# The two products of a chunked recurrence: odd chunks written to the other half of the partitions

## The chip, the cores and the metric

The kernel runs on one core of one Trainium2 chip. The metric is the device time of one execution in microseconds (us), the median of the runs shown. A profile is one further execution with the hardware profiler on; its own time is given beside it. PE is the matrix engine (TensorE), PEld its loading of weights, DVE the vector engine, ACT the scalar engine, POOL the GpSimd engine, SP the engine that issues most of the transfers.

## The reference, cut to what matters

One transformer block over 1024 positions and a width of 1024, in float32: a token mixer with two branches, softmax attention with forget gates (8 heads of 64) and an RWKV-7 recurrence (8 heads of 64), merged by gates, and then a convolutional feed-forward layer of width 2816. The change lies in the recurrence:

```python
def step(state, inp):
    r_t, w_t, k_t, v_t, a_t, b_t = inp
    sa = jnp.einsum('bhvk,bhk->bhv', state, a_t)
    state = state * w_t[:, :, None, :] + sa[..., None] * b_t[:, :, None, :] + v_t[..., None] * k_t[:, :, None, :]
    y_t = jnp.einsum('bhvk,bhk->bhv', state, r_t)
    return state, y_t

_, y = lax.scan(step, state0, (tm(r_h), tm(w_h), tm(k_h), tm(v_h), tm(a_vec), tm(b_vec)))
```

## The kernel before, in words

The recurrence is not run step by step. The sequence is cut into chunks of 64 positions (CH). A unit of work is one pair of heads `p` and one half `hf` of the sequence: 8 chunks (NCU) and two heads `h`, of which one stands on partitions 0 to 63 and the other on 64 to 127 (`HS[0]` and `HS[1]`). There are 4 pairs and 2 halves, so 8 units.

For each unit `pre` (from line 698) makes what belongs to the chunks alone: the masked products of keys, `E` (line 764); the inverse of a triangular matrix for each chunk, by substitution in blocks of 32 rows, 31 steps of two DVE instructions each (`t` and `E`, lines 784 and 786) between transfers through DRAM (`sm` to `M32` before them, `se` to `TT` behind them); transposes of values and queries into `UV` and `QA`; and `q` (line 822), whose matmuls read one half of the partitions and write the other.

`main` (from line 830) then finishes the unit:
- `xi` and `zi` (lines 850 and 857) complete the inverse; ACT copies the result into `TT` (line 859).
- The product with the inverse, `uw` (line 868): for each chunk and head a matmul of 64 rows, 64 output rows and 128 columns, `TT` by `QA`. Four chunks fill one PSUM bank of 512 columns, so two banks hold the unit. DVE copies the second half of each chunk's columns into `Wt` (line 870), ACT the first half into `UV` (line 872).
- The product of the step matrices, `mz` (line 880), of the same shapes: `Wt` by `E`. DVE adds to make `Zt` (line 882) and the step matrices `Mt` (line 884).
- `sp` and `yp` (lines 893 and 895) start the sums of states and outputs; they read `UV` and `E`.
- The walk over the chunks (lines 899 to 905): `sp` by `Mt` and the state before, and ACT makes the next state `S` (line 903).
- `yp` by `Zt` (line 910), and the group norm of the outputs (`mu`, `va` and what follows).

The banks of `uw`, `mz`, `xi`, `zi` and other short products come from one pool of four, `gen`. Every f32 matmul appears in the profile as two records.

Around this, PE's order is written out beforehand: `Weave` (line 49) counts a time for PE from a cost for each matmul (`mm_cost`, line 68), which goes by the shapes and types of the operands alone. `main` and `pre` are generators; a `yield` of a number asks that so many nanoseconds of other PE work be put in before the chain goes on, and that work is the projections (`ps_rkv`, `qk`, `v`, `gt`), which have banks of their own. Only PE's order is fixed by hand in this stage. The orders of DVE, ACT, POOL and SP are made by the scheduler of the language, from its own model of times. Behind the recurrence come the attention and the feed-forward layer.

Of the kernel before, what the change touches and what calls it, by code (L numbers as in the profile page):

```python
# [12 lines left out]
ALU = mybir.AluOpType  # L13
# [9 lines left out]
CH = 64  # L23
NCU = NH // CH
# [108 lines left out]
def hybrid_block(ctx: ExitStack, tc: tile.TileContext, a, out):  # L133
    nc = tc.nc
# [3 lines left out]
    def mm(o, lhsT, rhs, start, stop, more=False):  # L138

        weave.mm_cost(o, lhsT, rhs)  # L140
        nc.tensor.matmul(o, lhsT, rhs, start=start, stop=stop, skip_group_check=more)  # L141
# [8 lines left out]
    tt, stt, ts = nc.vector.tensor_tensor, nc.vector.scalar_tensor_tensor, nc.vector.tensor_scalar  # L150
# [195 lines left out]
    with ExitStack() as es:  # L346
# [7 lines left out]
        def gen(name):  # L354
            return pr.tile([128, NH], F32, tag="gen", name=name)
# [45 lines left out]
        HS = (slice(0, 64), slice(64, 128))  # L401
# [285 lines left out]
        Mt = rw.tile([128, NCU, 128], F32, name="Mt")  # L687
# [142 lines left out]
        def main(k, p, hf):  # L830
            o = units.pop((p, hf))
            n = f"{p}_{hf}"
            cs = slice(hf * NH, hf * NH + NH)
            pcd, ar, E, QA, TT, bon, UV = (o[k] for k in ("pcd", "ar", "E", "QA", "TT", "bon", "UV"))
# [25 lines left out]

            yield 2000
            Wt = rw.tile([128, NCU, CH], F32, tag="Wt", name=f"Wt{n}", bufs=1)
            for c0 in range(0, NCU, 4):
                ps = gen(f"uw{n}{c0}")
                for c in range(c0, c0 + 4):
                    for h in range(2):
                        x = (c - c0) * 128
                        mm(ps[HS[h], x : x + 128], TT[HS[h], c, :], QA[HS[h], c, :, :], start=True, stop=True)
                pv = ps.rearrange("p (c a s) -> p c a s", a=2, s=CH)
                nc.vector.tensor_copy(Wt[:, c0 : c0 + 4, :], pv[:, :, 1, :])  # L870
                for h in range(2):
                    nc.scalar.copy(UV[HS[h], c0 : c0 + 4, h, :], pv[HS[h], :, 0, :])
            yield 2970
            Zt = rw.tile([128, NCU, CH], F32, tag="Zt", name=f"Zt{n}", bufs=1)
            for c0 in range(0, NCU, 4):
                ps = gen(f"mz{n}{c0}")
                for c in range(c0, c0 + 4):
                    for h in range(2):
                        x = (c - c0) * 128
                        mm(ps[HS[h], x : x + 128], Wt[HS[h], c, :], E[HS[h], c, h, 1:3, :], start=True, stop=True)  # L880
                pv = ps.rearrange("p (c a s) -> p c a s", a=2, s=CH)
                tt(Zt[:, c0 : c0 + 4, :], pv[:, :, 0, :], ar[:, 1, c0 : c0 + 4, :], op=ALU.add)
                for h in range(2):
                    tt(Mt[HS[h], c0 : c0 + 4, HS[h]], pv[HS[h], :, 1, :],
                       ident[HS[h], HS[h]].unsqueeze(1).to_broadcast([64, 4, CH]), op=ALU.add)

            yp = py.tile([128, NCU, CH], F32, tag="yp", name=f"yp{n}")
# [87 lines left out]
        def main_chain():  # L975
            for k, (p, hf) in enumerate(order):
                while (p, hf) not in units:
                    yield 200
                yield from main(k, p, hf)
                yield 0  # L980
# [205 lines left out]
    def bank(k, name):  # L1186
        return pb.tile([128, NH], F32, tag="big", name=name) if k > 5 else pz.tile([128, NH], F32, tag=f"p{k}", name=name)
# [442 lines left out]
    ps = {t: [bank(k, f"wo{t}_{c}") for c, k in enumerate(ks)] for t, ks in enumerate(((0, 5), (6, 7), (1, 2)))}  # L1630
# [12 lines left out]
    def wo_do(t, k):  # L1643
        ps = [bank(k + c, f"wo{t}_{c}") for c in range(2)]
        for kt in range(KT):
            wo_mm(t, kt, ps)
        return ps

    ps = wo_do(3, 3)
# [7 lines left out]
    ps = wo_do(4, 0)  # L1657
# [15 lines left out]
    for t, k in ((5, 2), (6, 6), (7, 4)):  # L1673
        ps = wo_do(t, k)
# [229 lines left out]
    for s, k in enumerate(ORDER):  # L1904
        ps = banks[4:] if k in (7, 4, 2) else banks[0:4]
# [109 lines left out]
```

## Time and profile before

| what | value |
|---|---|
| median of 3 runs | 1662.81 us (1658.86 to 1663.45) |
| profiled execution, its own time | 1662.01 us |
| its span | 1660.2 us |
| mean granted clock | 0.989 |
| PE busy over the span | 1615.2 us (97%) |
| DVE busy over the span | 1223.2 us (74%) |
| ACT busy over the span | 822.3 us (50%) |

The profiled execution's own time is its span and 1.8 us around it. The first of the eight `uw` products begins at 235.4 us and the last at 576.6 us; the stretch from 230 to 606 us is the one to look at. A row of the order of time gives start, length, engine, line, operation, output and inputs, shapes and the number of records; a row of a tile gives the count and then shortest, median and longest duration in nanoseconds.

### The profile page before, as it was taken

The numbers are of one execution on the slowest core, as the hardware profiler recorded it, in microseconds if no ns is written. First come the engines' busy times: TensorE is split into PE (matmuls) and PEld (weight loads), VectorE is DVE, ScalarE is ACT, GpSimd is POOL, SyncE is SP. The second block draws the span as 40 slices with busy tenths as digits, with TensorE's granted clock in tenths as the row PEclk, the third lists the DMA queues.
The fourth block names the chain that finished last, engine by engine and source line by source line (L and its number), as shares of the span: only waits on it lengthen the run. The fifth ranks groups of instructions, "written<-read, shape, count | busy, mean of one in ns | idle before, by whom it ended". The sixth has DMA issues, their size and how long they took to land.

```text
span 1660.2 us, 25947 instructions
## 1 busy us (share of the span) xinstructions
PE 1615.2 (97%) x9694; PEld 1346.1 (81%) x9694; DVE 1223.2 (74%) x2371; ACT 822.3 (50%) x1540; POOL 130.3 (8%) x152
## 2 busy tenths in 40 slices
PE   7999999999999999999999999999999999999998
PEld 7777777898978788888778887888888888888886
DVE  5786787878876536888678347897777777786677
ACT  5563335444455656666623225654444444555455
POOL 0011001111111011221022000000000000000000
PEclk9999999999999999999999999999999999999999
DMA  8488645443343246433187411243223223574363
GB/s 336 139 322 238 177 116 140 131 121 97 100 115 97 96 129 153 124 114 110 64 323 265 166 70 58 66 138 108 96 95 120 97 96 108 208 266 156 125 209 108
DMA packets 121645, 240.59 MB, mean 145 GB/s; under 512 B 40048, under 2 KB 48880, under 8 KB 121520
## 3 DMA queue, kind: packets, MB, share of 16 engines
q1 hardware_dynamic: 113040, 220.58, 40.7%
q0 software_dynamic: 8480, 18.37, 4.2%
q8 instruction: 76, 1.25, 0.3%
q14 instruction: 49, 0.40, 0.1%
HBM read 173.35 MB, written 65.54 MB: 144 GB/s over the span
## 4 chain that ended last, share of the span: by engine, by line
PE 62%; DVE 3%; ACT 2%; DMA 1%; issue 1%; SPq 0%; ACTq 0%; DVEq 0%
PE X L141 14%; PE D L141 13%; PE Y L141 7%; PE wo L141 5%; PE br L141 5%; PE gt L141 4%; PE rk_ps L141 4%; PE W L141 3%; PE lg L141 2%; PE ov L141 2%; PE tp L145 2%; DVE nm L1049 1%; DVE P L1059 1%; DMA g<-d_gate 0%; DVE tl L1089 0%
## 5 line engine op out<-in xcount | busy, mean ns | idle before, releaser
L141 PE MATMUL D<-op,op 128*128 128x512 f32 x924 | 209.8, 389 | 0.0
L141 PEld LDWEIGHTS D<-op,op 128*128 128x128 f32 x924 | 173.3, 188 | 36.3 <-DVE op L1252 0.3
L141 PE MATMUL X<-T_m,S 128*128 128x512 f32 x440 | 106.9, 389 | 0.0
L141 PEld LDWEIGHTS X<-T_m,S 128*128 128x128 f32 x440 | 82.5, 188 | 17.5 <-ACT x L1542 0.4
L1251 ACT CAST op<-g 128x512 fp32r<-128x512 f32 x77 | 47.8, 621 | 72.1 <-PE D L141 47.8
L1252 DVE TENSOR_TENSOR op<-g,op 128x512 fp32r<-128x512 f32 x77 | 53.0, 688 | 41.1 <-ACT op L1251 41.1
L1502 DVE SCALAR_TENSOR_TENSOR c<-ab,vec,c 128x512 f32<-128x512 f32 x88 | 65.9, 749 | 18.4 <-ACT c L1505 16.8
L784 DVE TENSOR_TENSOR t<-E,M 128x60 f32<-128x60 f32 (+24 forms) x248 | 56.1, 226 | 26.6 <-DMA M<-sm 20.6
L274 DVE TENSOR_TENSOR lo_in<-raw_in,hi_in 128x512 fp32r<-128x512 f32 x84 | 57.7, 725 | 22.0 <-PE gt L141 7.2
L1466 DVE TENSOR_TENSOR A<-ur,A 128x512 fp32r<-128x512 f32 x64 | 43.9, 688 | 39.0 <-ACT A L1462 38.8
L1466 DVE TENSOR_TENSOR S<-ur,S 128x512 fp32r<-128x512 f32 x66 | 45.5, 691 | 35.2 <-ACT S L1462 35.1
L1462 ACT CAST S<-ur 128x512 fp32r<-128x512 f32 x66 | 41.0, 622 | 56.1 <-DVE ur L1455 30.9
L141 PE MATMUL Y<-T_h,S 128*128 128x512 f32 x264 | 65.6, 398 | 1.6 <-ACT T_h L1720 1.0
L141 PE MATMUL Y<-T_h,A 128*128 128x512 f32 x264 | 63.4, 389 | 0.0
L1053 ACT ACTIVATE P<-lg,nm 128x896 f32<-128x896 f32 (+3 forms) x64 | 47.4, 742 | 29.3 <-DVE nm L1049 19.6
L141 PEld LDWEIGHTS Y<-T_h,S 128*128 128x128 f32 x264 | 50.6, 192 | 13.4 <-ACT T_h L1720 1.8
L1462 ACT CAST A<-ur 128x512 fp32r<-128x512 f32 x64 | 39.6, 621 | 42.9 <-PE X L141 31.0
L141 PE MATMUL W<-B_f,A 128*128 128x512 f32 x252 | 60.6, 389 | 0.0
L786 DVE TENSOR_TENSOR E<-E,t 128x60 f32<-128x60 f32 (+24 forms) x248 | 55.8, 225 | 6.4
L141 PE MATMUL X<-B_b,A 128*128 128x512 f32 x252 | 60.5, 389 | 0.0
L141 PEld LDWEIGHTS Y<-T_h,A 128*128 128x128 f32 x264 | 49.5, 188 | 10.3
L272 ACT CAST hi_in<-raw_in 128x1024 fp32r<-128x1024 f32 x42 | 43.9, 1049 | 25.4 <-PE ps_rkv L141 11.3
(481 smaller groups left out, 4142.0 us busy)
## 6 DMA issues: line engine op xcount, KB each, us to landing
raw_in<-in_w_in SPq DMA_DIRECT2D x50, 512.0 KB, 3.9
wm<-in_w_mod SPq DMA_DIRECT2D x48, 512.0 KB, 6.7
ur<-in_w_up SPq DMA_DIRECT2D x44, 512.0 KB, 4.0
g<-d_g SPq DMA_DIRECT2D x35, 512.0 KB, 3.8
d_g<-gs SPq DMA_DIRECT2D x44, 256.0 KB, 2.0
d_g<-c SPq DMA_DIRECT2D x33, 256.0 KB, 4.3
d_st<-qh SPq DMA_DIRECT2D x64, 128.0 KB, 2.4
stA<-d_st POOLq DMA_DIRECT2D x8, 1024.0 KB, 6.2
```

The costliest lines, as they stand in the source:

```text
L141: nc.tensor.matmul(o, lhsT, rhs, start=start, stop=stop, skip_group_check=more)
L145: nc.tensor.transpose(o, i, eye)
L272: nc.scalar.copy(hi, raw)
L274: nc.vector.tensor_tensor(lo[:, c : c + NH], raw[:, c : c + NH], f32(hi[:, c : c + NH]), op=ALU.subtract)
L784: tt(tv, E32[:, 0:J, s : s + 1].to_broadcast([128, J, W]), M32[:, s : s + 1, s + 1 : 32].to_broadcast([128, J, W]), op=ALU.mult)
L786: tt(E32[:, 0:J, s + 1 : 32], E32[:, 0:J, s + 1 : 32], tv, op=ALU.add)
L1053: nc.scalar.activation(e[:, 0:n], lg[:, 0:n], AF.Exp, bias=nm[:, 0:1], accum_out=nm[:, 1:2])
L1251: nc.scalar.copy(hi, src)
L1252: tt(lo, src, f32(hi), op=ALU.subtract)
L1462: nc.scalar.copy(hi, src)
L1466: tt(lo, src, f32(hi), op=ALU.subtract)
L1502: stt(c, ab[:, x + hf * NH : x + hf * NH + NH], V("conv_w", 22 * x + i), c, op0=ALU.mult, op1=ALU.add)
```

## The change

In `uw` and in `mz` both banks are taken at the start, one for the even chunks and one for the odd ones, where before the first held chunks 0 to 3 and the second chunks 4 to 7. The matmuls of an even chunk write the half of the partitions that they read, as before; those of an odd chunk write the other half. The order of chunks and heads is the same, and so are the shapes. The evictions come after all 16 matmuls in the program. Those of an even chunk stay as they were but step over every second chunk; those of an odd chunk read one half of the partitions and write the other, and so `Wt` and `Zt` of the odd chunks take one instruction for each half: three instructions for a unit in place of two. `UV` and `Mt` already had one for each half; their number stays at four.

```diff
--- before.py
+++ after.py
@@ -860,28 +860,32 @@
 
             yield 2000
             Wt = rw.tile([128, NCU, CH], F32, tag="Wt", name=f"Wt{n}", bufs=1)
-            for c0 in range(0, NCU, 4):
-                ps = gen(f"uw{n}{c0}")
-                for c in range(c0, c0 + 4):
-                    for h in range(2):
-                        x = (c - c0) * 128
-                        mm(ps[HS[h], x : x + 128], TT[HS[h], c, :], QA[HS[h], c, :, :], start=True, stop=True)
-                pv = ps.rearrange("p (c a s) -> p c a s", a=2, s=CH)
-                nc.vector.tensor_copy(Wt[:, c0 : c0 + 4, :], pv[:, :, 1, :])
+            ps = [gen(f"uw{n}{e}") for e in range(2)]
+            for c in range(NCU):
                 for h in range(2):
-                    nc.scalar.copy(UV[HS[h], c0 : c0 + 4, h, :], pv[HS[h], :, 0, :])
+                    x = c // 2 * 128
+                    mm(ps[c % 2][HS[h ^ c % 2], x : x + 128], TT[HS[h], c, :], QA[HS[h], c, :, :], start=True, stop=True)
+            pv = [x.rearrange("p (c a s) -> p c a s", a=2, s=CH) for x in ps]
+            nc.vector.tensor_copy(Wt[:, 0::2, :], pv[0][:, :, 1, :])
+            for h in range(2):
+                nc.vector.tensor_copy(Wt[HS[h], 1::2, :], pv[1][HS[1 - h], :, 1, :])
+            for e in range(2):
+                for h in range(2):
+                    nc.scalar.copy(UV[HS[h], e::2, h, :], pv[e][HS[h ^ e], :, 0, :])
             yield 2970
             Zt = rw.tile([128, NCU, CH], F32, tag="Zt", name=f"Zt{n}", bufs=1)
-            for c0 in range(0, NCU, 4):
-                ps = gen(f"mz{n}{c0}")
-                for c in range(c0, c0 + 4):
-                    for h in range(2):
-                        x = (c - c0) * 128
-                        mm(ps[HS[h], x : x + 128], Wt[HS[h], c, :], E[HS[h], c, h, 1:3, :], start=True, stop=True)
-                pv = ps.rearrange("p (c a s) -> p c a s", a=2, s=CH)
-                tt(Zt[:, c0 : c0 + 4, :], pv[:, :, 0, :], ar[:, 1, c0 : c0 + 4, :], op=ALU.add)
+            ps = [gen(f"mz{n}{e}") for e in range(2)]
+            for c in range(NCU):
                 for h in range(2):
-                    tt(Mt[HS[h], c0 : c0 + 4, HS[h]], pv[HS[h], :, 1, :],
+                    x = c // 2 * 128
+                    mm(ps[c % 2][HS[h ^ c % 2], x : x + 128], Wt[HS[h], c, :], E[HS[h], c, h, 1:3, :], start=True, stop=True)
+            pv = [x.rearrange("p (c a s) -> p c a s", a=2, s=CH) for x in ps]
+            tt(Zt[:, 0::2, :], pv[0][:, :, 0, :], ar[:, 1, 0::2, :], op=ALU.add)
+            for h in range(2):
+                tt(Zt[HS[h], 1::2, :], pv[1][HS[1 - h], :, 0, :], ar[HS[h], 1, 1::2, :], op=ALU.add)
+            for e in range(2):
+                for h in range(2):
+                    tt(Mt[HS[h], e::2, HS[h]], pv[e][HS[h ^ e], :, 1, :],
                        ident[HS[h], HS[h]].unsqueeze(1).to_broadcast([64, 4, CH]), op=ALU.add)
 
             yp = py.tile([128, NCU, CH], F32, tag="yp", name=f"yp{n}")
```

## Prediction

> **What bounds the kernel now.** I read the page first, then the busy time of the stretch from 230 to 606 us, in which the recurrence runs, and after it the waits of that stretch.
>
> ```profile
> span 1660.2 us, 25947 instructions
> ...
> PE 1615.2 (97%) x9694; PEld 1346.1 (81%) x9694; DVE 1223.2 (74%) x2371; ACT 822.3 (50%) x1540; POOL 130.3 (8%) x152
> ```
>
> ```profile
> 230.00:606.00 376.00, 368.29 (x3651) 309.71 (x3650) 276.07 (x771) 188.88 (x368) 47.20 (x60) 1.00 0.39 110
> ```
>
> The numbers of the second row are length, then busy time of PE, PE's weight loads, DVE, ACT and POOL, and at the end the granted clock (1.00). PE stands still for 376.00 - 368.29 = 7.7 us of the stretch; whatever the recurrence leaves free, the woven-in projections fill. DVE has 100 us spare. So a microsecond taken from PE's own work is a microsecond of the whole, unless PE then meets a wait that does not move with it. The waits that it meets now are few:
>
> ```profile
> PE uw L141 <- ACT TT L859: 2.9, 2, 2.0
> PE v L141 <- DVE vs L955: 1.9, 3, 1.3
> PE sp L141 <- ACT S L903: 1.1, 1, 1.1
> ```
>
> (total, times, longest). None of them is for a PSUM bank of the two products, so taking both banks at the start of a product costs nothing that shows here.
>
> **The two products.** There are eight units (four head pairs, two halves), each with one uw and one mz product, 16 blocks in all:
>
> ```profile
> L141 PE MATMUL uw<-QA,TT x256: 269/269/418, 235.4 to 578.3; 64*64 64x128 f32 x128
> L872 ACT COPY UV<-uw x32: 344/367/369, 237.1 to 579.5; 64x256 f32<-64x256 f32 x32
> L870 DVE COPY Wt<-uw x16: 398/417/425, 236.7 to 578.6; 128x256 f32<-128x256 f32 x16
> ```
>
> ```profile
> L141 PE MATMUL mz<-E,Wt x256: 269/269/321, 240.7 to 583.6; 64*64 64x128 f32 x128
> L884 DVE TENSOR_TENSOR Mt<-mz,cst x32: 405/417/428, 242.2 to 585.7; 64x256 f32<-64x256 f32 x32
> L882 DVE TENSOR_TENSOR Zt<-mz,ar x16: 413/424/425, 241.9 to 584.9; 128x256 f32<-128x256 f32 x16
> ```
>
> 256 records in 8 units are 32 for 16 matmuls: an f32 matmul leaves two records, two passes. Here is one block in order of time (start, length):
>
> ```profile
> 235.41 1.96 PE L141 MATMUL uw<-QA,TT 64*64 64x128 f32 x32
> ...
> 236.69 0.42 DVE L870 COPY Wt<-uw 128x256 f32<-128x256 f32 x1
> ...
> 237.31 2.14 PE L141 MATMUL ps_rkv<-u_lo,hi_in 128*128 128x512 f32 x8
> ...
> 237.70 0.42 DVE L870 COPY Wt<-uw 128x256 f32<-128x256 f32 x1
> ```
>
> The last record starts 1.96 - 0.27 = 1.69 us after the first. Now the lucky place on which I rest most: in the seventh unit the product q, whose matmuls go from one half of the partitions to the other (the crossed pair of quarters), is directly followed by mz on the straight pair.
>
> ```profile
> 532.17 0.97 PE L141 MATMUL q<-UV,E 64*64 64x64 f32 x26
> ...
> 532.94 0.33 PE L141 MATMUL mz<-E,Wt 64*64 64x128 f32 x2
> 532.98 0.28 PE L141 MATMUL q<-UV,E 64*64 64x64 f32 x4
> ...
> 533.10 0.27 PE L141 MATMUL mz<-E,Wt 64*64 64x128 f32 x1
> ...
> 533.10 0.22 PE L141 MATMUL q<-UV,E 64*64 64x64 f32 x1
> 533.10 0.27 PE L141 MATMUL mz<-E,Wt 64*64 64x128 f32 x1
> ...
> 533.21 1.70 PE L141 MATMUL mz<-E,Wt 64*64 64x128 f32 x28
> ```
>
> Three things are in it. mz comes in pairs, the two quarters at once: two records at 532.94, two at 533.10, and then 28 records, 14 pairs, in steps of (1.70 - 0.27)/13 = 0.11. The first step is 0.16, since the first weight load lies open. And the last six records of q, on the crossed quarters, start at 532.98 to 533.11, after mz has begun: all four quarters run together, with q four records in 0.28 - 0.22 = 0.06 and mz's own steps no longer than elsewhere. The operands of q and mz share the rows of the array but not its columns. That such sharing costs nothing over many steps, and that two row halves can write two banks on the same partitions, these rows show:
>
> ```profile
> 242.81 0.29 PE L141 MATMUL yp<-E,UV 128*64 128x64 f32 x4
> 242.87 0.20 PEld L141 LDWEIGHTS sp<-UV,E 128*64 128x64 f32 x4
> 242.92 0.29 PE L141 MATMUL sp<-UV,E 128*64 128x64 f32 x4
> ...
> 256.58 1.16 PE L141 MATMUL p<-ar,bk 64*128 64x128 f32 x16
> ```
>
> sp and yp use two column halves over all rows and take 0.11 for four records of 64 columns; p uses two row halves over all columns, into two banks, and takes its 16 records of 128 columns in (1.16 - 0.27)/7 = 0.13 a pair with the open first load.
>
> **What the change saves on PE.** A block becomes eight rounds of four instead of 16 of two: the last round starts 0.16 + 6 x 0.11 = 0.82 after the first, and its second pair 0.01 later. Saved are 1.69 - 0.83 = 0.86 us a block, 16 x 0.86 = 13.8 us. The bounds are 0 (four quarters overlap only at such a seam) and 13.8 (the rounds cannot be shorter than one quarter's step); the seam shows the four together, so I take 13.8. The planner's cost of a matmul does not depend on the half it writes, so the order of PE's queue stays as it is.
>
> A rule of the Trainium skill speaks against this: its page TensorE: Matmul & The Clock Gate, in Part 3 (what overlaps and what doesn't), has matmuls start and end strictly in program order. By that rule the second pass of each matmul would hold back every later matmul, and the saving would be 0 in place of 13.8; the seam disagrees, since q's last six records start behind mz's first two.
>
> **What it adds.** One Wt copy and one Zt addition more in each unit, for the odd chunks have to change halves: 2 x 0.42 = 0.84 us of DVE, 6.7 in all, beside PE's work where there is room. ACT's four UV copies and DVE's four Mt additions stay in number and size. The even bank is full at 0.82 + 0.27 = 1.09 us into the block, exactly when the first bank (chunks 0 to 3) was before, so evictions begin as early; they end at most 0.42 later. But PE arrives at the next product 0.86 sooner. So each margin shrinks by 1.28 at the step from Wt to mz. The narrowest:
>
> ```profile
> 387.18 0.41 DVE L870 COPY Wt<-uw 128x256 f32<-128x256 f32 x1
> 434.83 0.42 DVE L870 COPY Wt<-uw 128x256 f32<-128x256 f32 x1
> 530.85 0.76 DVE L870 COPY Wt<-uw 128x256 f32<-128x256 f32 x2
> ```
>
> ```profile
> 388.13 1.96 PE L141 MATMUL mz<-E,Wt 64*64 64x128 f32 x32
> ...
> 435.70 1.96 PE L141 MATMUL mz<-E,Wt 64*64 64x128 f32 x32
> 437.59 0.34 PE L141 MATMUL sp<-UV,E 128*64 128x64 f32 x4
> ```
>
> ```profile
> 435.30 1.50 ACT L872 COPY UV<-uw 64x256 f32<-64x256 f32 x4
> ```
>
> In the fourth unit Wt ends 0.54 before mz, in the fifth 0.45, in the seventh 1.33. With 1.28 less the fourth waits 0.74 and the fifth 0.83; the seventh just doesn't. In the fifth UV ends at 436.80, 0.79 before sp; PE comes 2 x 0.86 - 0.83 = 0.89 sooner and UV 0.42 later, a wait of 0.52. Together 2.1 us. Queued behind these waits are the woven projection matmuls of PE, since its order is fixed.
>
> The second loss is where DVE, not PE, sets the pace. The chain that ended last shows it in the seventh unit:
>
> ```profile
> 530.43 2.92 DMA M<-sm
> ...
> 545.61 0.63 ACT gs L341
> 546.23 0.21 ACT S L903
> 546.49 0.43 PE sp L141 x2
> ```
>
> From the DMA to 546.49 it runs over DVE, in its queue order, and PE waits 1.1 at the end. Two blocks lie in that time on PE: their 2 x 0.86 = 1.72 are lost to the wait, and the 0.84 of DVE comes on top: 2.6 us. The three waits of v for vs are of the same kind: between 0 and 2.6; no row says how their chain begins, so I take 1.1, near the lower end, as they are waits of 0.6 on average.
>
> **Sum.** 13.8 - 2.1 - 2.6 - 1.1 = 8.0 us. The profiled execution took 1662.0 (its span and 1.8 around it) and becomes 1654.0, with a span of about 1652.2; the median of the three runs shown, 1662.8, is 0.8 higher, so I forecast 1654.8.
>
> **The rivals.**
> *No overlap of four over a whole block.* Then a block stays at 1.69, all evictions begin at its end and end up to 0.84 later, and the fourth and fifth units wait 0.30 and 0.39: 1662.8 + 0.7 = 1663.5. The seam speaks against it; for it, that q had only six records left there.
>
> *DVE takes the gain.* If four of the eight units behave as the seventh does, 4 x 2.6 + 2.1 = 12.5 are lost and the time is 1661.5. For it: DVE is busy 276 of 376 us and stands in queue order behind DMA waits. Against it: only one chain of that kind shows.
>
> *Slower: the order of the ACT and DVE queues.* That order is made by the scheduler and not by hand here, and with another one a copy can stand behind a long wait. It has happened once, at the second unit:
>
> ```profile
> 283.08 0.63 ACT L719 ACTIVATE el<-cum 128x512 f32<-128x512 f32 x1 [4.00 <-DVE cum L715]
> ```
>
> with the TT copies behind it, and uw waited for them. In the first unit Wt ended at 238.12, and the best margin that I read is some 2.6 us; less 1.28 it is 1.35. A wait of 4.00 ahead of the odd chunks' copies then costs 2.65 of PE. From five units on, 13.3, nearly all is spent, and in all eight it is 21.2 - 13.8 = 7.4 slower: 1670.2. Against it: no reason why all eight should be struck.
>
> *Slower: the weight load lies open at every change between straight and crossed quarters.* Then each of 7 changes in a block costs 0.16 - 0.11 = 0.05 and nothing is saved: 16 x 0.35 = 5.6, with the 0.7 above 1669.1. The loads of sp above (242.87) start while yp's matmuls run on the same rows, which speaks against it. The same section of that page of the Trainium skill says that a weight load overlaps a running matmul only on other rows of the array; those loads of sp disagree with it.
>
> **How the numbers follow.** About 0.3%, 5.0 us, is what a measurement of this kernel can tell from no change: faster is below 1657.8, slower above 1667.8. Chances: the forecast 0.66; no overlap 0.06 and DVE takes the gain 0.14, both within the bound; the queue order 0.10 and the open weight load 0.04, both slower. So faster 0.66, same 0.20, slower 0.14. The forecast's own range goes from no loss (1649.0, and 1 us for scatter: 1648.0) to 1657.8; the range over all takes in the two cases without effect, to 1664.0, and leaves out the slower ones.
>
> **What would show it.** Right: uw and mz blocks of about 1.10 in place of 1.96, with records in fours; Wt and Zt 24 times each; mz waiting for Wt in one or two units, and sp for ACT S for over 3 us at the seventh. PE busy some 12 us lower. Wrong: blocks still of 1.9 (no overlap), or of 2.2 and more (open loads); blocks of 1.1 with PE's idle time in the stretch up from 7.7 to near 20 (DVE or a queue took it).

## The result, and the profile after

Against runs of the kernel before on the same chip the change makes no difference that can be measured: 1661.53 us (median of 12 runs, 1658.15 to 1663.25) beside 1659.49 us (median of 12, 1658.38 to 1665.19), ratio 1.0004 with a 95% interval of 0.9994 to 1.0013 (taken over all the runs, not from the two medians). The first three of those 12 are the runs that the forecast counted from (1662.8), so its start lay 3.3 us above the median of all. The profiled execution took 1658.15 us. The 8.0 us that were forecast did not come, although PE's two products shrink as was said. The measured time lies in the range over all (to 1664.0) only because that range took in the cases without effect; the forecast itself, given a chance of 0.66 and a range that ended at 1657.8, missed. The page of the changed kernel:

```profile
span 1656.4 us, 25970 instructions
...
PE 1600.9 (97%) x9694; PEld 1328.8 (80%) x9694; DVE 1228.6 (74%) x2387; ACT 822.2 (50%) x1540; POOL 132.6 (8%) x152
```

PE has as many matmuls as before and 14.3 us less busy time (1615.2 - 1600.9); DVE has 16 instructions and 5.4 us more. The groups of the two products (smallest, median and largest ns, first and last start):

```profile
L141 PE MATMUL uw<-QA,TT x256: 269/269/320, 236.2 to 579.8; 64*64 64x128 f32 x128
L871 DVE COPY Wt<-uw x16: 417/422/427, 238.9 to 581.0; 64x256 f32<-64x256 f32 x16
L869 DVE COPY Wt<-uw x8: 415/418/425, 238.3 to 580.1; 128x256 f32<-128x256 f32 x8
```

```profile
L141 PE MATMUL mz<-E,Wt x256: 269/269/321, 240.6 to 584.3; 64*64 64x128 f32 x128
L888 DVE TENSOR_TENSOR Mt<-mz,cst x32: 403/422/428, 243.6 to 588.4; 64x256 f32<-64x256 f32 x32
L885 DVE TENSOR_TENSOR Zt<-mz,ar x16: 417/417/426, 244.5 to 587.6; 64x256 f32<-64x256 f32 x16
L883 DVE TENSOR_TENSOR Zt<-mz,ar x8: 414/417/419, 243.2 to 585.9; 128x256 f32<-128x256 f32 x8
```

Two numbers in them already hold the result. From the first record of uw to the last of mz the recurrence took 583.6 - 235.4 = 348.2 us before (rows in the prediction), and now 584.3 - 236.2 = 348.1. The 3.8 us between the two profiled spans (1660.2 and 1656.4) arise behind the recurrence: matched record by record, PE is 0.6 us later than before at 672 us and 3.8 earlier at 943 us, and between these the trace before has half clock at 682 and at 935 us, the trace after has none. PE's timeline shows the blocks that were made shorter:

```profile
236.17 1.10 PE L141 MATMUL uw<-QA,TT 64*64 64x128 f32 x32
...
240.64 1.10 PE L141 MATMUL mz<-E,Wt 64*64 64x128 f32 x32
```

1.10 in place of 1.96: 0.83 from the first record's start to the last one's, where it was 1.69. So 16 x 0.86 = 13.8 us of matrix work are gone, and the same stretch is as long as it was. The row of 230 to 606 us, and what PE waits for in it (total, times, longest):

```profile
230.00:606.00 376.00, 360.43 (x3655) 298.49 (x3652) 282.52 (x789) 188.47 (x368) 47.82 (x60) 0.99 0.39 110
```

```profile
PE sp L141 <- ACT S L907: 4.6, 4, 2.3
PE v L141 <- DVE vs L959: 2.8, 2, 1.8
PE uw L141 <- ACT TT L859: 2.3, 2, 1.6
PE va L141 <- POOL Wts L693: 1.8, 2, 1.1
```

PE stands still for 376.00 - 360.43 = 15.6 us, where it was 7.7. Matching each of PE's records between 231 and 606 us with its partner before gives the account: the blocks (the uw and mz products), with the waits that now fall inside them, are 11.4 us shorter and not 13.8 (2.4 lost); waits elsewhere are 9.3 longer; and steps that ran at half clock cost 2.0 more. 13.8 - 2.4 - 9.3 - 2.0 = 0.1.

**One place in full.** In the second unit the loss can be followed. PE after:

```profile
289.83 1.68 PE L141 MATMUL mz<-E,Wt 64*64 64x128 f32 x32
...
297.23 0.33 PE L141 MATMUL sp<-S,Mt 128*128 128x64 f32 x2
...
297.92 1.09 PE L141 MATMUL ps_rkv<-u_hi,hi_in 128*128 128x512 f32 x4
301.35 0.43 PE L141 MATMUL sp<-S,Mt 128*128 128x64 f32 x2 [2.34 <-ACT S L907]
301.60 1.89 PE L141 MATMUL ps_rkv<-u_hi,hi_in 128*128 128x512 f32 x4
```

and PE before:

```profile
291.79 1.96 PE L141 MATMUL mz<-E,Wt 64*64 64x128 f32 x32
...
299.47 0.33 PE L141 MATMUL sp<-S,Mt 128*128 128x64 f32 x2
...
301.08 0.33 PE L141 MATMUL sp<-S,Mt 128*128 128x64 f32 x2
```

mz starts 1.96 us earlier, the state walk's first step 2.24 earlier (297.23 beside 299.47), and its second step 0.27 later. All that was won is given back in one wait, for the state S. (Not all of it was won by the change: the kernel before runs at half clock from 286.1 to 289.5 us here, the one after not until 301.8.) What DVE and ACT did meanwhile, after (first the two rows of DVE, then those of ACT):

```profile
294.15 0.42 DVE L883 TENSOR_TENSOR Zt<-mz,ar 128x256 f32<-128x256 f32 x1
...
299.62 0.69 DVE L739 TENSOR_TENSOR bk<-kr,en 128x512 f32<-128x512 f32 x1
```

```profile
300.35 0.62 ACT L740 COPY bk<-bk 64x512 f32<-64x512 f32 x1 [3.22 <-DVE bk L739]
300.99 0.31 ACT L907 ACTIVATE S<-sp,pcd 128x64 f32<-128x64 f32 x1
```

and before:

```profile
292.93 0.42 DVE L882 TENSOR_TENSOR Zt<-mz,ar 128x256 f32<-128x256 f32 x1 [0.17 <-PE mz L141]
...
297.99 0.69 DVE L739 TENSOR_TENSOR bk<-kr,en 128x512 f32<-128x512 f32 x1
```

PE hands mz over earlier, but DVE begins to evict it 1.2 us later, since its queue has other work in front (the substitution steps t and E of a coming unit) and more Wt and Zt instructions of its own; bk, further down the same queue, comes 1.6 later; ACT's copy of bk waits for that, and S stands behind the copy. The busy row of these 18 us, before and then after, shows how little room DVE has here:

```profile
284.00:302.00 18.00, 17.46 (x172) 14.57 (x172) 17.17 (x50) 7.31 (x16) 1.02 (x5) 0.91 0.39 104
```

```profile
284.00:302.00 18.00, 14.62 (x169) 11.54 (x170) 17.29 (x51) 7.36 (x16) 1.24 (x4) 0.99 0.39 104
```

DVE, the third busy figure, is at 17.2 and 17.3 of 18. PE is busy for 2.8 us less, part of it because the row before holds the half clock (0.91), and the walk's second step comes no earlier.

### The profile page after: what moved, and what is told of

It is laid out like the page before. It is cut to its first block, busy times and chain, and to the rows that moved or that the text cites. A ratio compares the mean times of both kernels' runs of the same rounds, so it can differ in the third digit from the quotient of the medians.

```text
span 1656.4 us, 25970 instructions
## 1 busy us (share of the span) xinstructions
PE 1600.9 (97%) x9694; PEld 1328.8 (80%) x9694; DVE 1228.6 (74%) x2387; ACT 822.2 (50%) x1540; POOL 132.6 (8%) x152
## 4 chain that ended last, share of the span: by engine, by line
PE 60%; DVE 6%; ACT 2%; DMA 1%; issue 1%; SPq 0%; POOL 0%; DVEq 0%; ACTq 0%
PE X L141 13%; PE D L141 13%; PE Y L141 6%; PE wo L141 5%; PE br L141 5%; PE gt L141 4%; PE rk_ps L141 3%; PE W L141 3%; PE lg L141 2%; PE ov L141 2%; PE tp L145 2%; DVE P L1063 1%; DVE nm L1053 1%; DMA g<-d_gate 0%; DVE tl L1093 0%
```

## The experiments

Four theories stand in the expectations. A: PE now arrives at handovers before DVE, ACT or POOL have their part ready, because of the order in which their queues stand, and half clock follows the longer waits. B: each build gets another order of those queues from the scheduler, and the result is that order's luck. C: the pace of the recurrence is set by a chain over DVE, ACT and transfers, and PE's work is not its bound, full as PE looks. D: PE's work is the bound, and only the added evictions eat the saving.

Beside each median stands the ratio to the kernel before in the same comparison, with its 95% interval, and "length" is the time from the first record of uw to the last of mz in the profile, 348.2 before and 348.1 after.

**The uw product alone** (mz as before):

> Only the product with the inverse (uw) is changed; mz stays as in the kernel before. Theory A (handovers: PE saves 0.86 us in each changed block, and gives it back where it now meets DVE or ACT before they are done, with the half clock behind a long wait): half of the PE saving, 8 x 0.86 = 6.9 us, and the waits of mz for Wt and UV alone, so 1 to 4 us faster than before, 1656 to 1659 by the median of 12 runs. Theory B (the scheduler's new order of the ACT and DVE queues is the loss, and any edit draws another order): anywhere within 4 us of before on either side. Theory C (the recurrence goes at the pace of a chain of DVE and transfers, PE's work is not its bound): within 1 us of before.

Measured: 1661.92 us (11 runs), 1.0004 (0.9993 to 1.0014), length 349.8.

**The mz product alone** (uw as before):

> Only the product of the step matrices (mz) is changed; uw stays as in the kernel before. Theory A: Wt and UV are made as early as before, the margin before mz is kept, and only the later end of Zt and Mt counts; 3 to 6 us faster than before. Theory B: anywhere within 4 us of before. Theory C: within 1 us of before, and not faster.

Measured: 1658.13 us (12 runs), 0.9985 (0.9974 to 0.9996), length 346.0. The rows that carry the length:

```profile
L141 PE MATMUL uw<-QA,TT x256: 269/269/320, 237.2 to 578.7; 64*64 64x128 f32 x128
...
L141 PE MATMUL mz<-E,Wt x256: 269/269/320, 242.5 to 583.2; 64*64 64x128 f32 x128
```

By the length, half of the edit brings 2.2 us of its 6.9, the other half takes 1.6. The two add to -0.6 and the whole has -0.1, so neither half hides the gain of the other. For uw alone, C is right and A misses. For mz alone, C misses, which allowed no gain: it is 2.5 us faster by the ratio, 3.3 by the medians (1661.47 for the kernel before), at the lower edge of A's 3 to 6 or just under it.

**Everything but the crossing**: banks by parity and the split evictions, with the matmuls straight.

```diff
-  mm(ps[c % 2][HS[h ^ c % 2], x : x + 128], TT[HS[h], c, :], ...)
+  mm(ps[c % 2][HS[h], x : x + 128], TT[HS[h], c, :], ...)
-  nc.vector.tensor_copy(Wt[HS[h], 1::2, :], pv[1][HS[1 - h], :, 1, :])
+  nc.vector.tensor_copy(Wt[HS[h], 1::2, :], pv[1][HS[h], :, 1, :])
```

(and so in UV, mz, Zt and Mt)

> Banks by parity and the evictions in the same number and order as in the changed kernel (three Wt and three Zt instructions in a unit), but every chunk writes the half of the partitions that it reads, so that PE keeps its two quarters at once and its 1.69 us for a block. Theory A: PE's saving is gone and the later evictions stay, so slower than before by 2 to 6 us, though less than the 13.8 saved, since PE now comes later to each handover. Theory B: as in the changed kernel, within 2 us of it if the order of the queues comes out the same. Theory C: slower than before by the added DVE work, 6.7 us.

Measured: 1665.43 us (9 runs), 1.0020 (1.0006 to 1.0034), length 352.1. By the length, the evictions, the later hand-over of the first bank and the new order of the queues cost 3.9 us together, and crossing, with 13.8 us of PE's work taken away, gives back 4.0. The other 9.8 are not eaten by the evictions: D would have kept them. A's forecast holds (4.0 us slower by the medians), C's 6.7 is missed, and so is B's, within 2 us of the changed kernel (2.7 by the ratios).

This pair also tests B, for the scheduler gave this kernel and the changed one nearly the same order. The two profiles hold the same instructions of ACT in the same order, and of DVE's 2387 only 12 would have to move to make the orders alike; between the kernel before and the changed one it is 92 of the 2331 that can be matched. So at one order, PE's work falls by 13.8 us and the recurrence by 4.0. Matched record by record, the blocks are 11.5 us shorter, waits elsewhere 5.7 longer, and half clock costs 1.8 more.

**More filler ahead of the two handovers.**

```diff
+ t0 = weave.now
  ...                      # the matmuls of the product
+ weave.now = t0 + (weave.now - t0) / 2
- yield 2970
+ yield 3830
- yield 3400
+ yield 4260
```

> The changed kernel, with the planner told the true length of the two products (half of its cost for them) and the 0.86 us that each block saves put in as further projection work behind it (the waits of 2970 and 3400 ns become 3830 and 4260), so that PE comes to mz and to the walk over the chunks as late as in the kernel before. Theory A: the waits of PE for Wt, UV and S that are new go, its idle time from 230 to 606 us falls from 15.6 towards 8 us, and 6 to 11 us are gained over before: 1649 to 1654. Theory B: the order of the queues changes again; anywhere within 4 us of before. Theory C: within 1 us of before.

Measured: 1692.94 us (5 runs), 1.0181 (1.0159 to 1.0203), length 382.0. The planner stretched the recurrence by 34 us, and PE waits more and not less (8.7 us for S in seven places, 8.8 for X in two). It moved too much at once to say anything for or against A.

**Relief for DVE: the low parts of the weights on POOL** (in the kernel before and in the changed one):

```diff
- nc.vector.tensor_tensor(lo[:, c : c + NH], raw[:, c : c + NH], ...)
+ (nc.gpsimd if "relief" in marks else nc.vector).tensor_tensor(lo[...], raw[...], ...)
```

> The kernel before, with DVE relieved in the recurrence: the low parts of the projection weights (two subtractions of 128x512 for each weight tile, 0.69 us each on DVE) are made by POOL. Only to be set beside its partner with the change. DVE's busy time from 230 to 606 us should fall from 276 to about 245. All theories: within 5 us of before, with a gain of at most the 7.7 us for which PE stands still there, and a loss if POOL brings the low parts late.

> The changed kernel, with DVE relieved in the same way. Theory A (what PE saves is lost where DVE, with its queue order and its added work, is late at the handovers): with DVE relieved the saving shows, and this is 5 to 11 us faster than its partner without the change. Theory C (a chain of waiting times and transfers sets the pace, whatever DVE's load): within 2 us of its partner. Theory B (the scheduler's order is luck): within 4 us of its partner on either side.

Measured: 1688.53 us (4 runs), 1.0169 (1.0155 to 1.0183), length 372.0; with the change 1692.02 us (4 runs), 1.0194 (1.0180 to 1.0208), length 374.8. POOL went from 47 to 113 us busy between 230 and 606 us, DVE only from 276 to 264, and the length grew by 24 and 27 us, in ways that weren't followed up (one such subtraction takes POOL 1.29 us, the median of 46, beside 0.68 on DVE before). It was no relief, so it does not test C as meant; it shows once more that the changed kernel is not the faster of a pair.

**ACT's copy of bk on POOL**, so that S does not stand behind it:

```diff
- nc.scalar.copy(bk[64:128, :, 2, :], bk[64:128, :, 0, :])
+ nc.gpsimd.tensor_copy(bk[64:128, :, 2, :], bk[64:128, :, 0, :])
```

> The kernel before, with one copy for each unit (the third part of bk, line 740) moved from ACT to POOL, so that ACT's queue, and with it the next state S, no longer stands behind DVE's chain for bk. To be set beside its partner with the change. All theories: within 3 us of before.

> The changed kernel with the same copy moved to POOL. Theory A, in its narrow form (the largest of the new waits, PE's for the state S, comes from ACT's queue, where S stands behind the copy of bk, which waits for DVE): the wait of sp for S falls from 4.6 us to under 2.5, the half clock at 302 us goes with it, and this is 2 to 6 us faster than its partner without the change. Theory C: within 2 us of its partner. Theory B: within 4 us on either side.

Measured: 1661.94 us (9 runs), 1.0015 (1.0002 to 1.0028), length 349.5; with the change 1664.55 us (7 runs), 1.0025 (1.0012 to 1.0038), length 352.6. The wait for S in the changed one:

```profile
PE sp L141 <- ACT S L907: 4.6, 5, 2.0
```

4.6 us, as without this edit (4.6). So the bk copy, the last link in the place shown above, is not what keeps the gain away; something else is late next. The narrow form of A falls. DVE and ACT keep the order of the kernel before in the first of these runs, apart from the eight copies that left ACT, and no gain shows there either.

**PE's work less, with no instruction of DVE or ACT added**: in the kernel before, two matmuls of each projection product of the recurrence left out, which the planner still counts.

```diff
+ if "rec" in marks and n in (18, 20):
+     weave.mm_cost(ps, ww[:, k0 : k0 + 128], xx[:, kt, cs])
+ else:
      mm(ps, ww[:, k0 : k0 + 128], xx[:, kt, cs], ...)
```

> The kernel before, with two of the 24 matmuls of each 512-column projection product in the recurrence left out (part of the low-order terms; the planner still counts them). About 33 products of that kind lie there, so PE saves 66 x 0.22 = 14.5 us in the same stretch as the change, spread evenly, and no instruction of DVE or ACT is added or made later. Theory D (PE's work is the bound, and only the added and later evictions of the change eat its saving): 10 to 14 us faster than before. Theory C (PE's work is not the bound in this stretch, each handover is soon late when PE gets faster): 0 to 5 us faster, and the waits of PE rise by most of what is saved.

Measured: 1660.33 us (11 runs), 0.9996 (0.9985 to 1.0008), length 345.5. The saving on PE was larger than I had counted: the page has 9598 matmuls in place of 9694, and 96 at 0.215 (from six of them in 1.52 us and four in 1.09) are 20.6 us. Of these 96, 62 (13.3 us) lie between the first record of uw and the last of mz, nearly what the change takes away there; 26 lie ahead of them and 8 behind. Its busy row of 230 to 606 us, PE's waits there, and the rows of the length:

```profile
230.00:606.00 376.00, 359.40 (x3563) 299.16 (x3562) 275.02 (x772) 190.61 (x371) 47.34 (x62) 0.99 0.38 108
```

```profile
PE sp L141 <- ACT S L906: 4.7, 4, 2.8
PE q L141 <- DVE QA L814: 3.5, 2, 2.5
PE va L141 <- POOL Wts L696: 3.0, 4, 1.6
```

```profile
L141 PE MATMUL uw<-QA,TT x256: 269/269/473, 234.1 to 574.7; 64*64 64x128 f32 x128
...
L141 PE MATMUL mz<-E,Wt x256: 269/269/320, 239.4 to 579.6; 64*64 64x128 f32 x128
```

PE stands still for 16.6 us, and the first wait is again sp for S, by 4.7 us, though no instruction of DVE or ACT was added. This is the changed kernel's picture without the change. The recurrence is 2.7 us shorter for 13.3 us less work, and the time as a whole is the same. C forecast this, and D misses. The order isn't held here, though: 209 of the 2347 DVE instructions that can be matched would have to move, so this run alone doesn't rule out B.

**PE's work more**: in the kernel before, the first bank's eight matmuls of each product issued twice, the second time uncounted by the planner.

```diff
- for c in range(c0, c0 + 4):
-     ...
+ for again in range(2 if c0 == 0 else 1):
+     t0 = weave.now
+     for c in range(c0, c0 + 4):
+         ...
+     weave.now = t0 if c0 == 0 and again == 0 else weave.now
```

> The kernel before, with the matmuls of the first bank of each of the 16 products issued twice (the second time over the first, the same result; not counted by the planner), so PE has 16 x 0.88 = 14.1 us more in the same places where the change saves 13.8. Evictions are the same in number. Theory D: 12 to 15 us slower. Theory C: the waits of PE shrink with it, so 4 to 10 us slower.

Measured: 1676.19 us (4 runs), 1.0089 (1.0074 to 1.0105), length 363.8.

```profile
L141 PE MATMUL uw<-QA,TT x384: 269/269/320, 238.2 to 595.8; 64*64 64x128 f32 x192
...
L141 PE MATMUL mz<-E,Wt x384: 269/269/320, 244.4 to 602.0; 64*64 64x128 f32 x192
```

256 more records in pairs of 0.11 are 14.1 us, and the length grows by 15.6, the median by 15.5. D forecast this (12 to 15 us) and C didn't (4 to 10), while the run before and the straight pair above went against D. So more work on PE costs all of itself here, and less work brings little; C holds for a saving and not for an addition. That fits a kernel at a corner between two bounds, PE's work and a pace of the other engines only a few us below it. It isn't shown: the doubled matmuls stand in the chain from uw to the state walk, so they would also lengthen a chain of handovers that leads through PE. More work elsewhere on PE, in the projections, was not tried.

**The Zt additions behind the state walk's yield**, so that Mt, which the walk needs, is evicted first; in the changed kernel, and with mz alone changed:

```diff
- tt(Zt[:, 0::2, :], ...)        # and the odd chunks' two
  ...
  yield 3400
+ tt(Zt[:, 0::2, :], ...)        # and the odd chunks' two
```

> The changed kernel with the three Zt additions written behind the wait ahead of the walk over the chunks, so that DVE's chain for bk, on which ACT's copy of bk and behind it the state S wait, goes ahead of them. If DVE's three Zt additions in that place are what holds S (the narrow form of theory A): the wait of sp for S falls from 4.6 us to about 2, and 2 to 5 us faster than the changed kernel. If the chain is held anyway: within 2 us of it.

> Only mz changed, as in the second run, with the Zt additions written later in the same way. Narrow theory A: 1 to 3 us faster than that run, 1655 to 1658, which would be the fastest of all. Otherwise within 1.5 us of it.

Measured: 1662.75 us (11 runs), 1.0012 (0.9999 to 1.0025), length 349.2; and 1658.42 us (11 runs), 0.9984 (0.9972 to 0.9997), length 347.7. PE waits 4.9 us for S in the first, 4.4 in the second: the order of Mt and Zt is not the link either. mz alone, with Zt early or late, is the fastest version found, some 2.5 us below the kernel before.

## Why the prediction was wrong where it was

**"So a microsecond taken from PE's own work is a microsecond of the whole": this step failed.** It was read from PE standing still 7.7 of 376 us and DVE having 100 to spare. Those two numbers tell at most that PE can't be made later for free; how much earlier it can be made before the others are late, they don't tell. Adding 14.1 us cost 15.5; taking 20.6 away in the projections brought 0.4 at the median; and taking 13.8 in these blocks brought nothing beside the kernel before, and 4.0 of the recurrence's length at an equal order of DVE and ACT. The rest went into waits of PE and half clock. DVE's 100 us are an average, too: from 284 to 302 us it has 0.8 to spare.

**Four quarters overlap: right.** The block has 0.83 from first to last start as forecast. The rule cited from the Trainium skill's page TensorE: Matmul & The Clock Gate, Part 3, that matmuls start and end strictly in program order, would have left 1.69; the blocks of the trace disagree. The open weight load, another rival of the prediction, would have made them longer; it did not come either.

**What is added: right.** Wt and Zt have 8 + 16 rows each at 0.42, Mt still has 32.

**The narrow places behind uw: about right in sum, not one by one.** Forecast were waits of 0.74 in the fourth unit, 0.83 and 0.52 in the fifth, none in the seventh, 2.1 together. The timeline after has, in those three units:

```profile
389.20 1.01 PE L141 MATMUL mz<-E,Wt 64*64 64x128 f32 x14 [0.17 <-DVE Wt L871]
...
436.65 0.43 PE L141 MATMUL mz<-E,Wt 64*64 64x128 f32 x4 [0.34 <-DVE Wt L869]
437.74 1.09 PE L141 MATMUL mz<-E,Wt 64*64 64x128 f32 x28 [0.66 <-ACT UV L874]
...
534.62 1.15 PE L141 MATMUL q<-UV,E 64*64 64x64 f32 x32 [0.46 <-ACT UV L874]
...
536.17 1.09 PE L141 MATMUL mz<-E,Wt 64*64 64x128 f32 x28 [0.17 <-ACT E L818]
```

```profile
436.96 1.52 ACT L874 COPY UV<-uw 64x256 f32<-64x256 f32 x4
...
533.82 0.74 ACT L874 COPY UV<-uw 64x256 f32<-64x256 f32 x2 [0.82 <-DVE Wt L869]
```

That is 1.80, of which the two in the seventh unit were overlooked. Neither mz nor this q reads the UV that line 874 writes: mz reads Wt and E, and q belongs to the next unit, whose UV comes from `vt`. But line 874 also empties the banks of uw. q starts right after its first two copies end (533.82 + 0.74 = 534.56), and mz's 28 records right after the first two of four (436.96 + 0.76 = 437.72); these two empty the bank of the even chunks. So the waits fit a bank of `gen` that isn't free yet. The prediction read that no wait is for a bank of the two products, "so taking both banks at the start of a product costs nothing that shows here"; that was so before the change and left these waits out. In the fifth unit the bank costs little, as Wt itself was ready only at 437.63; by this reading q's 0.46 is all due to it.

**"sp for ACT S for over 3 us at the seventh": wrong.** It waits 1.12 there, as long as before (1.1); its unit had been held up by other waits on the way. The loss came at state walks that showed no wait before, of the first and second units above all (1.0 and 2.5 us), and at the products that wait for Wts, vs and q. The term "DVE sets the pace" was put at one chain with 2.6 us, and v's waits at 1.1; 3.7 in all were forecast, and 9.3 us of waits between blocks were measured, and 2.4 inside them.

**A term that was not in the sum: the clock.** The rows around 301 us show it: the four projection matmuls that took 1.09 just before the wait of 2.34 take 1.89 just after it, and the busy row there has the granted clock at 0.50:

```profile
301.80:305.20 3.40, 3.40 (x10) 2.72 (x10) 3.40 (x7) 1.25 (x3) 1.58 (x1) 0.50 0.62 143
```

At half clock some half of the 3.4 us is lost to PE, about 1.7. Of such stretches there are two within the recurrence after, one before.

**The rival that came.** *DVE takes the gain* gave 12.5 us lost and 1661.5; 13.7 were lost, and the median is 1661.5. That the two times agree is luck, since the rival counted from 1662.8 and the kernel before has 1659.5 in this comparison. Its premise (four units like the seventh) isn't what happened: the waits are spread over S, vs, Wts, UV, Wt and q, and not DVE alone is late but ACT and POOL behind it. What was held against it, that only one chain of that kind showed, was no evidence: a wait that is just covered doesn't show. The sign named beforehand, blocks of 1.1 with PE's idle time up from 7.7 toward 20, is what the trace has (15.6).

**What stays open.** Which chain sets the pace isn't settled. Taking the bk copy or Zt out of S's way moved nothing; that there are several chains, each within some us of the next, fits this but isn't shown. The four banks of `gen` are one more candidate: in the run with less PE work, q's longest wait for QA (2.5 us) fits a bank, too (line 814 there empties that of `at`, and q does not read QA), and no run freed banks earlier. B can't be the loss of 9.8 us between the straight pair, whose orders are nearly equal; it isn't excluded where orders differ, so 2 us between the kernel before and another one can be that order. That mz alone gains and uw alone doesn't fits with uw's results being read within 2 or 3 us and mz's later, but this is argued and not shown.

## What to carry to other kernels

That an engine is 98% busy doesn't show that work taken from it is time saved. Before an edit that shortens its work, take a like amount of other work from it, and nothing else, and look: here that one run (0.9996) would have told that 13.8 us less on PE bring little, whatever the edit. And read the spare time of the next engine in the places where the two meet, not over the stretch.

## What was not expected of the hardware

f32 matmuls on 64x64 quarters, straight and crossed, run four at a time: 16 of them, 32 records, take 0.83 from first to last start, 0.11 a round of four, which is what a round of two takes.

A wait of 2.3 us was enough for a stretch at half clock of 3.4 us, and the place of the wait matters as much as its length. In the trace after, the stretches at 226.7, 301.8 and 448.6 us start 22 and 43 times 3.413 us apart, and in the 3.4 us that end at each start PE stood still for 2.2, 2.3 and 1.8 us. In the run with less PE work, whose stretches keep the same step (228.4, 542.4, 675.5 us: 92 and 39 times 3.413), a longer wait, 2.46 us up to 318.2, was followed by none: it falls into two of these steps, with 1.4 and 1.1 us. The Trainium skill's page TensorE: Matmul & The Clock Gate, Part 1, has a free-running window of about 3.4 us and an idle window of that length before the clock falls; the length of the half-clock stretch agrees, the idle time that it took was shorter here.

Most of the scatter between runs of one kernel goes with that clock: over the 27 runs of the kernel before in the last comparison the time rises by 1.0 us for each 0.001 that the mean granted clock falls (correlation -0.77), about one such stretch more (0.5 x 3.4 / 1660 = 0.001). The kernel with less PE work has a median clock of 0.987 beside 0.992, so by that line about 5 us of what it saved went into half clock; drawn by such lines to the same clock of 0.990 it is 6 us faster (1656.8 beside 1662.9), which is still under a third of 20.6; its profiled span and the one before, both at 0.989, differ by 3.2. The changed kernel has 0.991, so there the clock explains only about 1 us.
